# Average pooling over 512 MB: each 64 KB-per-partition load issued as two DMAs of half its columns

## The chip, the cores and the metric

The kernel runs on one core of one Trainium2 chip. The metric is the device time of one execution in microseconds (us). Three executions of the kernel before took 1558.53, 1558.62 and 1558.92 us, so its time is the median, 1558.62 us.

## The reference

The input x is a float32 array of 64 x 256 x 8192 elements (536.87 MB). Each output element is the mean of four neighbouring elements of the last axis, and the windows do not overlap:

```
kernel_size = stride = 4
out_len = (length - kernel_size) // stride + 1          # 2048
for i in range(out_len):
    start = i * stride
    output[:, :, i] = np.mean(x[:, :, start : start + kernel_size], axis=2)
```

The output is 64 x 256 x 2048 float32 (134.22 MB). Since 8192 is a multiple of 4, no window crosses a row, and the whole input may be treated as one flat run of numbers, of which every four make one output.

## The kernel before, in words

The flat input is cut into 32 groups. In a group, each of the 128 partitions owns one unbroken run of 32768 input elements (128 KB) and the 8192 outputs (32 KB) that come from it. A group is worked in two steps, so there are 64 steps, counted here from load 0 to load 63.

One step loads half of every partition's run: 16384 columns, 64 KB per partition, 8.39 MB in all, into a tile `xt` (line 70). The tiles `xt` come from a pool with two buffers, so load n+2 goes to the buffer of load n and cannot be issued before VectorE (DVE) has read that buffer for the last time. All DMAs, loads and stores alike, are issued by SyncE (SP) on one queue, in program order: an issue that waits holds up every issue behind it. Each DMA is carried out by 16 DMA engines side by side, each of which moves 8 of the 128 partition rows, one packet per row.

The work on a tile is the helper `pool`. DVE adds neighbouring pairs and writes the sums into the front half of the same tile (line 51), then adds neighbouring sums into the output tile `ot` (line 56). ScalarE (ACT) multiplies that part of `ot` by a quarter in place (line 57). The output tiles have two buffers of their own. One store of 4.19 MB, 32 KB per partition, writes a whole group (line 74). It is issued one group late: SP issues the store of group g-1 right behind the second load of group g. So from the second group on the queue holds, again and again: load, load, store.

The last step differs. Its load is issued as two DMAs of 11264 and 5120 columns (`LAST`), DVE and ACT work on the two pieces separately, and the outputs of the last group leave in three stores (lines 76 and 81). These two loads are called the tail pieces below.

The program that is built counts the completion of DMAs on eight semaphores in turn. The issue of a DMA therefore also waits until the DMA eight places before it has completed.

Of the kernel before, what the change touches and what calls it, by code (L numbers as in the profile page):

```python
# [1 line left out]

# [4 lines left out]

ADD = mybir.AluOpType.add

LOAD = 16384  # L10
PER_STORE = 2
LAST = (11264, 5120)


@with_exitstack
def kernel(
    ctx: ExitStack,
    tc: tile.TileContext,
    x: bass.AP,
    kernel_size: bass.AP,  # L20
    stride: bass.AP,
    out: bass.AP,
):

    nc = tc.nc
    K = int(kernel_size)
    assert K == 4 and int(stride) == 4 and x.shape[-1] % 4 == 0
    P = nc.NUM_PARTITIONS  # L30
    dt = x.dtype
    inv_k = 1.0 / K

    run = LOAD * PER_STORE
    total = x.shape[0] * x.shape[1] * x.shape[2]
    groups = total // (P * run)
    assert groups * P * run == total and groups >= 2
    xg = x.flatten_outer_dims().rearrange("r l -> (r l)").rearrange("(g p w) -> g p w", p=P, w=run)
    og = out.flatten_outer_dims().rearrange("r l -> (r l)").rearrange(
        "(g p w) -> g p w", p=P, w=run // K  # L40
    )

    pin = ctx.enter_context(tc.tile_pool(name="xin", bufs=2))
    pout = ctx.enter_context(tc.tile_pool(name="res", bufs=2))

    def pool(xt, at, width, ot, to):


        half = width // 2
        four = xt[:, at : at + width].rearrange("p (m k) -> p m k", k=2)  # L50
        nc.vector.tensor_tensor(  # L51
            out=xt[:, at : at + half], in0=four[:, :, 0], in1=four[:, :, 1], op=ADD
        )
        two = xt[:, at : at + half].rearrange("p (m k) -> p m k", k=2)
        o = ot[:, to : to + width // K]
        nc.vector.tensor_tensor(out=o, in0=two[:, :, 0], in1=two[:, :, 1], op=ADD)  # L56
        nc.scalar.mul(o, o, inv_k)  # L57

    tiles = {}
    for n in range(groups * PER_STORE):  # L60
        g, j = divmod(n, PER_STORE)
        last = n == groups * PER_STORE - 1
        if j == 0:
            tiles[g] = pout.tile([P, run // K], dt, name="ot")
        ot = tiles[g]
        xt = pin.tile([P, LOAD], dt)
        spans, at = [], 0
        for w in LAST if last else (LOAD,):
            lo = j * LOAD + at
            nc.sync.dma_start(out=xt[:, at : at + w], in_=xg[g][:, lo : lo + w])  # L70
            spans.append((at, w))
            at += w
        if j == PER_STORE - 1 and g > 0:
            nc.sync.dma_start(out=og[g - 1], in_=tiles.pop(g - 1)[:, :])
        if last:
            nc.sync.dma_start(out=og[g][:, : j * LOAD // K], in_=ot[:, : j * LOAD // K])
        for at, w in spans:
            to = (j * LOAD + at) // K
            pool(xt, at, w, ot, to)
            if last:  # L80
                nc.sync.dma_start(out=og[g][:, to : to + w // K], in_=ot[:, to : to + w // K])


# [1 line left out]
_INS = ['x', 'kernel_size', 'stride']  # L85
_OUTS = [((64, 256, 2048), 'float32')]

_NUMBERS = {'kernel_size': 4, 'stride': 4}


# [26 lines left out]
```

## Time and profile before

| What | Value |
|---|---|
| median of three executions | 1558.62 us |
| the profiled execution: its own time | 1558.32 us |
| the profiled execution: span from first to last instruction | 1556.5 us |
| moved by DMA | 671.12 MB, mean 431 GB/s |
| DVE busy | 839.8 us (54% of the span) |
| ACT busy | 232.9 us (15%) |

The profiled execution spends 1.82 us outside its span. Busy shares are averages over the whole span. Besides the views of the page, the trace keeps one record for each packet that a DMA engine handled: when it started, how long it took, and its size. A packet of a load here is one partition's 64 KB; a packet of a store is one partition's 32 KB; and each DMA ends on each of the 16 engines with one packet of 4 bytes that counts up its semaphore.

### The profile page before, as it was taken

To read this page: it belongs to the slowest core of one execution; us is meant where nothing else is said; L and a number is where in the kernel's file an instruction comes from. 1 tells how busy PE (TensorE), PEld (TensorE's weight loads), DVE (VectorE), ACT (ScalarE), POOL (GpSimd) and SP (SyncE) were. 2 spreads that over 40 slices of the span, in tenths; PEclk is the share of its full clock that TensorE was granted. 3 is DMA by queue.
4 is the path that set the end of the run, shared out by engine and by line. 5 is a ranking of instruction groups with operands and counts; after the bars stand their busy time and mean duration, and the time that the engine had idled before them with its cause. 6 is when DMAs were issued, how large, how long until landed. Compare 5 with 4: busy or idle time off the path is not lost.

```text
span 1556.5 us, 463 instructions
## 1 busy us (share of the span) xinstructions
DVE 839.8 (54%) x130; ACT 232.9 (15%) x66; POOL 0.2 (0%) x4
## 2 busy tenths in 40 slices
DVE  3645645456454564545645556545465454654546
ACT  1101111111111111111111111010110101101011
POOL 0000000000000000000000000000000000000000
DMA  9999999999999999999999999999999999999999
GB/s 416 445 406 431 431 435 440 431 429 433 423 441 433 431 431 425 440 431 431 435 436 435 437 435 435 428 432 435 431 433 440 428 441 436 433 431 425 440 429 389
DMA packets 14259, 671.12 MB, mean 431 GB/s; under 512 B 1584, under 2 KB 1584, under 8 KB 1712
## 3 DMA queue, kind: packets, MB, share of 16 engines
q1 hardware_dynamic: 14256, 671.09, 99.9%
q14 instruction: 3, 0.02, 0.0%
HBM read 536.87 MB, written 134.22 MB: 431 GB/s over the span
## 4 chain that ended last, share of the span: by engine, by line
DMA 72%; DVE 27%; issue 0%; ACT 0%; SPq 0%
DMA xt<-in_x_dram 72%; DVE xt L51 18%; DVE ot L56 9%; ACT ot L57 0%; SPq L70 0%
## 5 line engine op out<-in xcount | busy, mean ns | idle before, releaser
L51 DVE TENSOR_TENSOR xt<-xt 128x8192 f32<-128x8192 f32 (+1 forms) x65 | 556.5, 8561 | 699.9 <-DMA xt<-in_x_dram 699.8
L57 ACT ACTIVATE ot<-ot 128x4096 f32<-128x4096 f32 (+1 forms) x65 | 231.6, 3564 | 1311.2 <-DVE ot L56 1311.2
L56 DVE TENSOR_TENSOR ot<-xt 128x4096 f32<-128x4096 f32 (+1 forms) x65 | 283.4, 4360 | 3.9
L57 ACT ACT_TABLE_LOAD x1 | 1.3, 1283 | 0.7 <-PEq L98 0.7
L98 POOL MEMSET const-bfloat16-1.0<- 128x1 bf16 x1 | 0.1, 101 | 0.0
L98 POOL MEMSET const-uint8-127<- 128x1 uint8 x1 | 0.1, 101 | 0.0
L98 POOL MEMSET const-float32-0.0<- 128x1 f32 x1 | 0.1, 98 | 0.2 <-issue 0.2
L98 POOL MEMSET const-float32-1.0<- 128x1 f32 x1 | 0.1, 98 | 0.0
## 6 DMA issues: line engine op xcount, KB each, us to landing
out_dram<-ot SPq DMA_DIRECT2D x31, 4096.0 KB, 41.2
xt<-in_x_dram SPq DMA_DIRECT2D x1, 5632.0 KB, 29.1
xt<-in_x_dram SPq DMA_DIRECT2D x1, 2560.0 KB, 34.8
out_dram<-ot SPq DMA_DIRECT2D x1, 2048.0 KB, 17.1
out_dram<-ot SPq DMA_DIRECT2D x1, 1408.0 KB, 12.2
xt<-in_x_dram SPq DMA_DIRECT2D x63, 35.2
out_dram<-ot SPq DMA_DIRECT2D x1, 640.0 KB, 10.7
```

What stands on the lines that cost most here:

```text
L51: nc.vector.tensor_tensor(out=xt[:, at : at + half], in0=four[:, :, 0], in1=four[:, :, 1], op=ADD)
L56: nc.vector.tensor_tensor(out=o, in0=two[:, :, 0], in1=two[:, :, 1], op=ADD)
L57: nc.scalar.mul(o, o, inv_k)
L98: nc = _bacc.Bacc("TRN2", target_bir_lowering=False, num_devices=1)
```

## The change

Every load but the last one, which already consists of two DMAs, is issued as two DMAs, of columns 0 to 8191 and of columns 8192 to 16383 of the tile. The tile, its buffers, the sums, the multiplication and the stores stay as they were. DVE's first addition on a tile still covers all its 16384 columns, so it waits for both DMAs.

```diff
 LOAD = 16384
 PER_STORE = 2
+HALVES = (8192, 8192)
 LAST = (11264, 5120)
...
         xt = pin.tile([P, LOAD], dt)
-        spans, at = [], 0
-        for w in LAST if last else (LOAD,):
+        at = 0
+        for w in LAST if last else HALVES:
             lo = j * LOAD + at
             nc.sync.dma_start(out=xt[:, at : at + w], in_=xg[g][:, lo : lo + w])
-            spans.append((at, w))
             at += w
         if j == PER_STORE - 1 and g > 0:
             nc.sync.dma_start(out=og[g - 1], in_=tiles.pop(g - 1)[:, :])
         if last:
             nc.sync.dma_start(out=og[g][:, : j * LOAD // K], in_=ot[:, : j * LOAD // K])
-        for at, w in spans:
+        at = 0
+        for w in LAST if last else (LOAD,):
             to = (j * LOAD + at) // K
             pool(xt, at, w, ot, to)
             if last:
                 nc.sync.dma_start(out=og[g][:, to : to + w // K], in_=ot[:, to : to + w // K])
+            at += w
```

## The prediction

> **What bounds the kernel now.** I read the page's head first, for who is busy all the time.
>
> ```profile
> span 1556.5 us, 463 instructions
> DVE 839.8 (54%) x130; ACT 232.9 (15%) x66; POOL 0.2 (0%) x4
> DMA packets 14259, 671.12 MB, mean 431 GB/s; under 512 B 1584, under 2 KB 1584, under 8 KB 1712
> q1 hardware_dynamic: 14256, 671.09, 99.9%
> ```
>
> No compute engine is near full, but the packets of the one queue fill 99.9% of the time of 16 DMA engines. The kernel is bound by the time of its packets: 12672 of data and 1584 of 4 bytes (99 DMAs times 16).
>
> The chain of waits seems to tell another story, so I read it second:
>
> ```profile
> 1391.12 8.70 DVE xt L51
> ...
> 1399.84 4.43 DVE ot L56
> ...
> 1404.29 35.15 DMA xt<-in_x_dram
> ...
> 1439.47 8.70 DVE xt L51
> ```
>
> Here DVE is on the path for 13.15 us of each 48.35. But that is only the path of one buffer. A load takes 35.15 us from issue to landing because it stands in the queue behind the rest of the other load and, in half of the cases, a store. The question is how much work is queued when a load is issued, and the order of time answers it:
>
> ```profile
> 1439.47 8.69 DVE L51 TENSOR_TENSOR xt<-xt 128x8192 f32<-128x8192 f32 x1 [6.14 <-DMA xt<-in_x_dram]
> 1448.19 4.42 DVE L56 TENSOR_TENSOR ot<-xt 128x4096 f32<-128x4096 f32 x1
> 1452.65 0.33 SPq L70 DMA_DIRECT2D xt<-in_x_dram  x1
> 1452.65 3.62 ACT L57 ACTIVATE ot<-ot 128x4096 f32<-128x4096 f32 x1 [15.68 <-DVE ot L56]
> 1456.30 0.34 SPq L74 DMA_DIRECT2D out_dram<-ot  x1
> 1468.47 8.69 DVE L51 TENSOR_TENSOR xt<-xt 128x8192 f32<-128x8192 f32 x1 [15.85 <-DMA xt<-in_x_dram]
> ```
>
> The load issued at 1452.65 finds another load that lands only at 1468.47, so 15.8 us of work is still ahead of it. The tightest places are the starts, before there are stores: the load issued at 55.1 us finds 6.2 us of work (DVE sits idle 6.19 us, until 61.30). So the queue never runs dry, and a DMA's latency costs nothing; what a change does to the sum of packet times comes out one to one.
>
> Third, the rate by stage, with the boundaries laid on landings (81.72, 617.41 and 1487.82 are starts of L51 in the chain, each behind the second load of a group):
>
> ```profile
> 81.72:617.41 535.69, 288.60 (x44) 79.55 (x22) 0.00 (x0) 1.00 1.00 432
> 617.41:1487.82 870.41, 472.22 (x73) 130.18 (x36) 0.00 (x0) 1.00 1.00 434
> ```
>
> In the second stage 18 rounds of load, load, store take 870.41 us, 48.356 each. In the first stage 11 rounds take 535.69 us, 3.77 more than 11 x 48.356, though the DMA share is 1.00 in both. By the packet records the 3.77 us sit in single slow packets, mostly the last load packet ahead of a store, which take 2.5 to 3.6 us instead of 2.418 on most engines about once per round, and nearly cease after some 740 us.
>
> **What a packet costs.** The packet records of the same execution give durations by size. Load packets of 64 KB: 2418 ns at the least and in most cases. Store packets of 32 KB: 1213. The tail pieces' load packets: 45056 bytes 1665 at the least, 1668.7 on average; 20480 bytes 761 and 764.3. The semaphore packets: 9. A data packet starts 4 ns before the one ahead of it on its engine has ended (3 ns beside a semaphore packet), so from start to start these are 2414, 1209 and 6 ns. Two packets of 32 KB thus take 2 x 1209 - 2414 = 4 ns more than one of 64 KB: a packet has a small fixed cost.
>
> The records also time whole DMAs, as the mean over the engines from one DMA's semaphore packet to the next one's. After 620 us, a load behind a store takes 19.320 us, a load behind a load 19.346, mean 19.333; a store takes 9.684. Check: 19.320 + 19.346 + 9.684 = 48.350, against the 48.356 above. The tail pieces take 13.328 and 6.093.
>
> **The change part by part.**
>
> *Packets and semaphores, on the bounding path.* 63 loads become 126 DMAs. That adds 63 x 16 = 1008 semaphore packets and 63 x 128 = 8064 data packets; on each engine, 9 packets per load. No row shows a 32 KB load, so I bound it per split load. From below by the store, which has the size but the other direction: 2 x 9.684 - 19.333 = +35 ns. From above by the tail pieces, which have the direction and are one load in two DMAs: 13.328 + 6.093 - 19.333 = +88 ns. Times 63: +2.2 to +5.5 us. Within this I build from the floor and the excess over it. The floor for half a load is 8 x 1209 + 6 = 9678 ns. The excess per packet of the tail pieces is 3.3 ns (20480 bytes) and 4.2 (45056) while DVE works, which it does nearly all through these two loads, and 1.3 while it does not. In the rounds DVE works during 3.5 us of the first and 13.15 of the second load, 43% of 38.7. So 0.43 x 3.7 + 0.57 x 1.3 = 2.3 ns, half a load takes 9678 + 8 x 2.3 = 9696 ns, and a split load 19.393 us, +60 ns. Times 63 this is **+3.8 us**. I take it because it goes by load packets, at the rounds' own mix.
>
> *The slow packets of the first stage* come at the turn from loads to stores, and the turns remain. I leave their 3.77 us as they are; bounds are that they vanish (-3.8) or double (+3.8), as the records do not say what makes or ends them.
>
> *SP's issues.* 63 more at 0.33 us each, 20.7 us of SP, which waits far longer:
>
> ```profile
> SPq L70 <- DVE ot L56: 817.2, 62, 13.2
> SPq L70 <- DMA xt<-in_x_dram: 549.3, 62, 21.0
> SPq L74 <- ACT ot L57: 101.9, 31, 3.3
> ```
>
> The second half is issued 0.33 us behind the first, whose 9.7 us of packets cover it. A store behind it waits for ACT's 3.62 us in any case (3.3 us in the third row) and loses nothing to 0.33. On the path of the end: 0.
>
> *The eight semaphores.* Five instead of three DMAs per round use them up faster. I went through the new order: what stands eight places ahead of an issue is always a DMA queued ahead of load n when load n+2 is issued, or load n itself or older (the first half of load 7, for example, waits for store 0, queued ahead of load 4). The issue waits for DVE's work on load n anyway, so the new waits are over by then: 0. If one were not, it would first eat the 6.2 or 15.8 us of queued work.
>
> *DVE's wait* for two DMAs instead of one: the second half lands last, where the whole load landed before. SP's extra wait instructions on line 70 are 17 ns each; one such on DVE per tile is covered by the 6.14 to 15.9 us that it sits idle: 0. ACT, the stores and the tail are untouched.
>
> **Sum.** 1558.32 + 3.8 = 1562.1 us for an execution like the profiled one. The median of the runs shown stands 0.30 above the profiled one, so I predict 1562.4 us, 0.24% slower.
>
> **A rule against the rows.** The Trainium skill, "DMA: Bandwidth & Descriptors", section "Anatomy of one DMA", gives a DMA a fixed cost of about 2.0 us beside its bytes and puts most of it down to the confirmation of the last write; the page measured it on GpSimd's path. Paid for each of the 63 added DMAs it would be an estimated +126 us, 1684 us in all. The row that bears on it is the spacing of queued DMAs here: between a load's last data packet and the next DMA's first on an engine lie a few ns, so such a cost is overlapped as long as the queue holds work. [...] The halves step by 128 KB from row to row, as the loads do already, and the tail's 20 KB pieces at that pitch ran at 20480 B / 764.3 ns = 26.8 GB/s per engine against 27.1 for whole loads.
>
> **The rivals.**
> 1. *The slow packets go away* (not slower). Half-size packets shift the engines against each other, and the first stage runs like the second. For it: the stage did end by itself, and the spread of one DMA's semaphore packets over the engines grew from 0.5 us to 3 in that time. Against: nothing ties the ending to packet size. It gives 3.8 - 3.8 = 0, 1558.6 us; from 0.7 us saved the outcome is within 0.2%.
> 2. *They grow or last.* Doubled they give 1566.2 us; going on through the 20 later rounds at 3.77 / 11 = 0.34 us each they add 6.9 us: 1569.3 us. For it: 16 engines that stay in step. Against: 18 rounds without.
> 3. *The queue runs dry at the half's boundary.* The first load landed 21.9 us after issue where queued ones take 19.33, so an exposed start costs some 2.6 us; 63 of them make 1726 us. Against: the cover above.
> 4. *The change does not do what it says.* If engines cut 64 KB up already, nothing moves but 63 x 6 ns = 0.4 us: 1559.0. Against: the records show single packets of 65536 bytes.
>
> **How the numbers follow.** 0.2% of 1558.6 us is 3.1 us, about what a measurement here can tell from no change; the forecast's +3.8 stands close above it. Forecast with its bounds (+2.2 to +5.5, 1560.8 to 1564.1): 0.68, of which I put 0.57 above 3.1 and 0.11 below. Rival 1: 0.16, same. Rival 2: 0.09, slower. Rivals 3 and 4: 0.01 each. Left for a gain that I can't name: 0.05 (rival 1 with the lowest packet cost gives 2.2 - 3.8 = -1.6 us, still within 0.2%). Together: slower 0.67, same 0.28, faster 0.05. The range leaves out the lower half of rival 1 and the gains below, and the upper half of rival 2 above: 1558.2 to 1567.0.
>
> **What would show it.** Right: the queue's packets rise from 14256 to 14256 + 8064 + 1008 = 23328 at 99.9%; rounds after 620 us of 48.36 + 0.12 = 48.48 us; load packets at 1213 to 1217 ns; DVE's busy time unchanged; its waits for loads 3 to 6 us longer in total. Wrong: a DMA share under 99%, a late round far from 48.48, or a first stage whose excess over its late rounds is not near 3.8 us.

## The result and the profile after

The changed kernel takes 1562.41 us (median of 10 executions, 1561.64 to 1562.74), the kernel before 1558.46 us on the same chip (median of 10, 1557.76 to 1558.95). The ratio is 1.0025 with a 95% interval of 1.0017 to 1.0034: slower by a quarter of a percent. The profiled execution after has a span of 1560.3 us and took 1562.08; before it was 1556.5 and 1558.32.

The head of the page after, with the DMA lines:

```profile
span 1560.3 us, 591 instructions
DVE 839.8 (54%) x130; ACT 233.0 (15%) x66; POOL 0.2 (0%) x4
DMA packets 23333, 671.14 MB, mean 430 GB/s; under 512 B 2592, under 2 KB 2592, under 8 KB 2720
q1 hardware_dynamic: 23328, 671.10, 100.0%
```

The compute engines did the same work, the queue's packets rose from 14256 to 23328, and their time still fills the span. The bound did not move. DVE's idle time in front of its loads grew by 3.9 us in total (columns: us in total, times, longest us; before, then after):

```profile
DVE xt L51 <- DMA xt<-in_x_dram: 699.8, 63, 22.6
DVE xt L52 <- DMA xt<-in_x_dram: 703.7, 63, 22.6
```

The order of time for one round shows that the queue did not run dry either:

```profile
1112.24 4.43 DVE L57 TENSOR_TENSOR ot<-xt 128x4096 f32<-128x4096 f32 x1
1116.70 0.80 SPq L71 DMA_DIRECT2D xt<-in_x_dram  x2
1116.70 3.62 ACT L58 ACTIVATE ot<-ot 128x4096 f32<-128x4096 f32 x1 [15.66 <-DVE ot L57]
1120.35 0.34 SPq L74 DMA_DIRECT2D out_dram<-ot  x1
1132.69 8.69 DVE L52 TENSOR_TENSOR xt<-xt 128x8192 f32<-128x8192 f32 x1 [16.02 <-DMA xt<-in_x_dram]
```

The two issues take 0.80 us together, end before ACT has finished, and the store is issued right after ACT, as before. The other load lands only at 1132.69, so 16 us of work lay ahead of the halves when they were issued.

The stages, with the boundaries on landings as in the prediction:

```profile
81.94:616.94 535.00, 288.60 (x45) 79.58 (x22) 0.00 (x0) 1.00 1.00 432
616.94:1491.56 874.62, 472.23 (x72) 130.22 (x36) 0.00 (x0) 1.00 1.00 432
```

The first 11 rounds of load, load, store take 535.00 us, 0.69 less than before. The next 18 take 874.62, 4.21 more. The start (up to the landing of load 3) and the end add 0.22 and 0.06. These four make the 3.8 us between the spans. So the kernel lost more in its regular rounds than the total shows, and gained a part of it back where the slow packets had been.

The packet records, averaged over the 16 DMA engines, separate this better, because a landing follows the slowest engine alone:

| Mean over the engines | before | after |
|---|---|---|
| late round (median of the last 14 of 28) | 48.350 us | 48.504 us |
| what the 28 rounds take above 28 late ones | 2.50 us | 1.39 us |
| end of the last packet on the slowest engine, behind the mean engine | 1.75 us | 1.95 us |

### The profile page after: what moved, and what is told of

The parts are those of the page before. It is cut to its first block, busy times and chain, and to the rows that moved or that the text cites. A ratio compares the mean times of both kernels' runs of the same rounds, so it can differ in the third digit from the quotient of the medians.

```text
span 1560.3 us, 591 instructions
## 1 busy us (share of the span) xinstructions
DVE 839.8 (54%) x130; ACT 233.0 (15%) x66; POOL 0.2 (0%) x4
## 3 DMA queue, kind: packets, MB, share of 16 engines
q1 hardware_dynamic: 23328, 671.10, 100.0%
## 4 chain that ended last, share of the span: by engine, by line
DMA 71%; DVE 27%; SPq 1%; issue 0%; ACT 0%; DVEq 0%
DMA xt<-in_x_dram 71%; DVE xt L52 18%; DVE ot L57 9%; SPq L71 1%; ACT ot L58 0%; DVEq L52 0%
```

## The experiments

The experiments ran on three chips on which the kernel before takes 1557.36, 1557.47 and 1557.46 us. Each run is compared with the kernel before on its own chip, not with 1558.46.

**Packets or DMAs?** The change doubles both. Theory P: what is paid for is the packet. Theory D: much of it is the DMA, by its semaphore packet and by something that happens where one load DMA follows another. Two kernels have the small packets without the added DMAs, in all loads but those of the last group (62 of 64). In each, step j takes every second piece of a partition's run, so that one DMA has rows that are broken up in DRAM; the results go to the matching parts of `ot`. With `SEGS = 2`:

```diff
+        segs = g < groups - 1
+        if segs:
+            nc.sync.dma_start(
+                out=xt[:, :].rearrange("p (a w) -> p a w", a=SEGS),
+                in_=xg[g].rearrange("p (a j w) -> p a j w", a=SEGS, j=PER_STORE)[:, :, j, :],
+            )
...
+        two = xt[:, :half].rearrange("p (a m k) -> p a m k", a=SEGS, k=2)
+        o = ot[:, :].rearrange("p (a j m) -> p a j m", a=SEGS, j=PER_STORE)[:, :, j, :]
```

> One DMA per load again, but its packets are of 32 KB: in groups 0 to 30, step j takes the two 8192-column pieces j and j+2 of each partition's run, so a row is two separate pieces in DRAM; the sums go to the matching quarters of the output tile. 62 loads. Theory P (the cost belongs to packets: 4 ns for each added one, and some 4 ns more for each load packet beyond the first sixteen behind a store): 32 + 34 = 66 ns per load, 4.1 us, less about 0.9 that the changed kernel gains in the first stage: near 1561.7 us, late rounds of 48.49 us. Theory D (beyond 4 ns per packet the cost belongs to the DMA: a semaphore packet and a slowdown that starts where one load DMA follows another): 32 ns per load, 2.0 us, less 0.9: 1559.5 to 1560.5 us, late rounds of 48.42 us.

Measured: 1561.48 us against 1557.36, ratio 1.0026 (1.0016 to 1.0035). That is 4.1 us more, where theory P gave 3.2 and theory D 1.0 to 2.0. The page has the packets of the changed kernel but the semaphores of the one before:

```profile
DMA packets 22195, 671.12 MB, mean 430 GB/s; under 512 B 1584, under 2 KB 1584, under 8 KB 1712
q1 hardware_dynamic: 22192, 671.09, 99.9%
```

Late rounds take 48.501 us, in the changed kernel 48.504. Theory P's 48.49 holds, theory D's 48.42 does not: with the DMAs undone and the packets kept, the whole cost stays. The rounds decide here, as the totals also hold the start, the slow packets and the end.

With `SEGS = 4`:

> As the run with one DMA and 32 KB packets, with four pieces of 4096 columns per load: 16 KB packets. Theory P: 32 packets of 607 ns from start to start per engine give 112 ns per load, and the slowdown per packet some 100 more: 212 x 62 = 13.2 us, near 1571 us, late rounds of 48.78 us. Theory D: 112 x 62 = 6.9 us, near 1565 us, late rounds of 48.58 us.

Measured: 1569.15 us, ratio 1.0076 (1.0064 to 1.0089), late rounds of 48.802 us. Again theory P's 48.78 and not theory D's 48.58. The total alone would not have told: it lies between theory P's 1571 and theory D's 1565, because the slow packets, treated below, cost less here. The next kernel makes the same 16 KB packets with four DMAs per load:

```diff
-HALVES = (8192, 8192)
+HALVES = (4096, 4096, 4096, 4096)
```

> The changed kernel with four DMAs of 4096 columns for each load but the last: the same 16 KB packets as the run with one DMA and 16 KB packets, and three more DMAs per load. Theory P: three semaphore packets of 6 ns more per load than that run, 63 x 18 ns = 1.1 us above it, near 1572.5 us. Theory D: three boundaries of about 40 ns more per load, 7.6 us above it. Both give some 14 us above the kernel before.

Measured: 1570.34 us, ratio 1.0083 (1.0069 to 1.0097), 1.2 us above the run with one DMA. Both pages count their packets:

```profile
DMA packets 38067, 671.12 MB, mean 428 GB/s; under 512 B 1584, under 2 KB 1584, under 8 KB 1712
q1 hardware_dynamic: 38064, 671.09, 100.2%
```

```profile
DMA packets 41478, 671.16 MB, mean 428 GB/s; under 512 B 4608, under 2 KB 4608, under 8 KB 4736
q1 hardware_dynamic: 41472, 671.11, 100.2%
```

The first fence is the page of the run with one DMA per load, the second that of the run with four. The 1.2 us are about what theory P gave (1.1), but not for its reason. The late rounds are the same, 48.802 and 48.797 us, though there are six more DMAs in each. In the profiled executions the mean engine ends at 1564.75 and 1564.79 us; what differs is the slowest engine, 1.07 us behind the mean in the one and 2.37 in the other. In the rounds an added DMA costs nothing that can be seen.

The three sizes make a line. Per round and engine there are 24, 40 and 72 data packets of loads and store, and a round takes 48.350, 48.50 and 48.80 us. That is 9.5 ns per added packet between the first two and 9.3 between the last two.

**What the 9.5 ns are.** Between two sizes, 4 ns are the fixed cost of a packet: 2 x 1209 - 2414 from start to start. The rest is in the excess of load packets over their least duration. I put the late load packets in order of their place behind the last store (ns above 2418 and above 1213, means over engines and rounds):

```
64 KB packets (before):  first load   0.0 0.0 0.0 0.0 0.0 0.1 0.4 1.0
                         second load  1.0 1.0 2.4 3.0 3.5 3.7 3.8 4.9
32 KB packets (after):   load, 1st half 0.0 0.0 0.1 0.6 0.1 0.3 0.5 0.7
                         load, 2nd half 0.7 1.0 2.6 3.0 4.0 4.7 4.2 3.9
                         next, 1st half 3.3 2.2 2.7 3.8 4.4 4.5 4.2 4.1
                         next, 2nd half 3.5 2.0 2.6 3.9 4.4 4.3 7.1 6.4
```

The first eight load packets behind a store have next to no excess, and the next eight climb to about 4 ns. From there on it stays near 4 ns, but falls back to about 2 on the second packet of each further DMA (places 18 and 26 in the changed kernel, place 18 alone in the run with one DMA and 32 KB). In these rounds the climb goes by the number of packets, not by time or bytes: it begins at the same places with 64 KB and with 32 KB, though that is 19 us behind the store in the one and 10 in the other. In the run with one DMA and 32 KB packets it begins at the same place too, so it does not need a DMA's boundary. The falls explain why added semaphore packets don't show: a late round's excess sums to 96 ns in the changed kernel and 113 with one DMA of the same packets, to 201 with four DMAs of 16 KB and 229 with one. These 17 and 28 ns less stand against two and six semaphore packets more of 6 ns each.

The place is not the whole of it. In the kernel before, the packets at places 11 to 16 average only 0.0 to 0.6 ns in the rounds that end between 230 and 760 us (slow packets left out), and near 3.5 only after some 900 us; in the changed kernel the packets from place 13 on have 1.2 to 3.9 ns in the earlier stretch as well. What decides that is not known. Nor does the excess follow DVE: the load packets of the changed kernel that ran wholly beside DVE averaged 2.6 ns of excess, those that ran wholly without DVE 2.8.

Runs that leave out the stores of the first 31 groups, and so most of the output, test whether the store is what resets it, and at the same time whether the slow packets of the first stage belong to stores:

```diff
-            nc.sync.dma_start(out=og[g - 1], in_=tiles.pop(g - 1)[:, :])
+            tiles.pop(g - 1)
```

> The kernel before without the stores of groups 0 to 30, so most of the output is left out. Question 1, the slow packets of the first stage. Theory T (they belong to the turn from loads to stores): none behind the first packets, two loads take the same time from the start. Theory S (they belong to the first 700 us of an execution, whatever runs): load packets of 2.5 us and more keep coming until some 700 us. Question 2, the few ns that load packets take above their floor: if a store resets them and they rise with the packets since, each packet is 4 to 5 ns above the floor of 2418 throughout, and two loads take 2 x (8 x 2418.3 + 6) = 38.70 us. Whole run near 1254 us.

> The changed kernel without the stores of groups 0 to 30. Two loads take 2 x (16 x 1213.2 + 12) = 38.85 us if all packets stand 4.2 ns above their floor, 0.15 us more than in the loads-only run with 64 KB packets, as in the kernels with stores (48.50 against 48.35). If the semaphores of the extra DMAs are free, as one and four DMAs at 16 KB suggested, 38.84. Whole run near 1259 us.

Measured: 1257.68 us with 64 KB and 1262.97 with 32 KB. Both are some 4 us above the expected totals; the spacing of the loads is what the question rests on. Two lines of the chain of waits of each, 64 KB first; the columns are start, duration and what:

```profile
907.63 25.50 DMA xt<-in_x_dram
...
946.33 25.50 DMA xt<-in_x_dram
```

```profile
911.19 25.20 DMA xt<-in_x_dram
...
950.03 25.22 DMA xt<-in_x_dram
```

Two loads take 946.33 - 907.63 = 38.70 us and 950.03 - 911.19 = 38.84 us, the expected numbers. The path runs through every second load, so from one line to the other two loads pass. After the first 300 us, load packets stand 3.8 ns (64 KB) and 4.2 ns (32 KB) above their least duration on average: without stores, the excess is there all the time. Why load packets behave so remains open.

**The slow packets.** In the loads-only run with 64 KB, 62 load packets were more than 2% above 2418 ns, 40 of them in the first 100 us, of which 16 are the first packet of each engine; three came after 300 us. In the kernel before there were 176, and more than 20 in every 100 us up to 600. Theory T holds for the most part: they belong to the turn from a load to a store, but for some at the very start. The next run asks whether they need engines that are in step, by putting some engines behind with four small loads ahead of the first:

```diff
+        if n == 0:
+            p0 = 0
+            for rows in (8, 4, 2, 1):
+                nc.sync.dma_start(out=ot[p0 : p0 + rows, :4096], in_=xg[0][p0 : p0 + rows, :4096])
+                p0 += rows
```

> The kernel before with four small loads of 8, 4, 2 and 1 rows of 16 KB ahead of the first load, into an output tile that is overwritten later: they put engine 0 about 2.4 us behind engines 8 to 15, engine 1 1.8, engines 2 and 3 1.2, engines 4 to 7 0.6. Theory K (the slow packets of the first stage need engines that are in step): the first twelve rounds lose their 2.4 us over 48.35 each; 0.6 us for the small loads and about 1 us for an engine that ends later come on top: 0.5 to 1.5 us below the kernel before. Rival (the slow packets have another cause and go on as they did): 1 to 2 us above it.

Measured: 1559.91 us, ratio 1.0017 (1.0008 to 1.0026). That is 2.4 us above the kernel before; the rival had 1 to 2 above, theory K 0.5 to 1.5 below. But the rounds speak for theory K: the first twelve together take 0.35 us more than 12 x 48.35, where the kernel before takes 2.40 more. The slow packets did mostly go. What ate the gain was the start and the end. The first load lands, on the mean engine, at 25.25 us against 21.99, where I expected 0.6 us; and the slowest engine ends 3.35 us behind the mean, 1.60 more than before. DVE's first addition, in the kernel before and here, shows the start on the slowest engine:

```profile
22.63 8.69 DVE L51 TENSOR_TENSOR xt<-xt 128x8192 f32<-128x8192 f32 x1 [22.63 <-DMA xt<-in_x_dram]
28.39 8.69 DVE L51 TENSOR_TENSOR xt<-xt 128x8192 f32<-128x8192 f32 x1 [28.39 <-DMA xt<-in_x_dram]
```

The second try puts the small loads behind load 1 (`if n == 2`, ahead of load 2's tile):

> The four small loads of the skewed kernel, but issued behind load 1, where the queue holds work, so that the first load is not late by 3.3 us as there. Theory K (the slow packets need engines that are in step): the first twelve rounds lose some 2.0 of their 2.4 us; 0.56 us for the small loads and about 1.4 us for a slowest engine that ends further behind the mean (2.8 us in the skewed run against 1.4 before) come on top: within 0.5 us of the kernel before. If the 3.3 us of the start did not account for the skewed run's loss, 2 us above it again.

Measured: 1560.06 us against 1557.46, ratio 1.0016 (1.0007 to 1.0025): 2.6 us above and not within 0.5. The first twelve rounds lose even more of their excess (0.18 us is left), but the small loads delay load 2 by 3.5 us on the mean engine here too. By the records their 16 KB packets take 0.7 to 1.7 us instead of the 0.611 of a 16 KB store packet, and while they run, most first packets of load 2 take 4 to 5.2 us instead of 2.418. The small loads all go to partitions 0 to 14; whether that is the reason wasn't tried.

**The cover taken away.** The prediction costs the added DMAs' latency at nothing because work is always queued. With one input buffer, no load is queued while DVE works:

```diff
-    pin = ctx.enter_context(tc.tile_pool(name="xin", bufs=2))
+    pin = ctx.enter_context(tc.tile_pool(name="xin", bufs=1))
```

> The changed kernel with one input buffer instead of two, so that the queue holds no load while DVE works: the cover is taken away. A load then costs 19.39 us of packets, 13.15 us of DVE and the latency of a DMA that nothing covers. With 2.6 us, from the first load's landing of the kernel before: 35.1 us per load, near 2260 us in all. The second half's DMA follows the first in the queue, so against the run with one buffer and 64 KB it costs only its packets, 0.06 us per load, 4 us. If each DMA had an own latency there, 2 us and more per load, 130 us.

> The kernel before with one input buffer, to set beside the changed kernel with one buffer (2283.67 us, 23.2 and 21.8 us of DVE's idle time per load). If the second half's DMA costs only its packets even where nothing covers a DMA's latency: 63 x 0.06 = 4 us below that, near 2280 us. If each DMA had a latency of its own of 2 us and more: some 130 us below, near 2150 us. Every turn from a load to a store should show slow last load packets here too, since the engines set out together at each load.

Measured: 2283.67 us with halves and 2282.88 with whole loads, one run of each. The lines of the order of time are, first with halves and then with whole loads, DVE's last work on a tile and its first on the next:

```profile
1029.27 4.43 DVE L57 TENSOR_TENSOR ot<-xt 128x4096 f32<-128x4096 f32 x1
...
1055.45 8.69 DVE L52 TENSOR_TENSOR xt<-xt 128x8192 f32<-128x8192 f32 x1 [21.76 <-DMA xt<-in_x_dram]
```

```profile
1029.89 4.43 DVE L56 TENSOR_TENSOR ot<-xt 128x4096 f32<-128x4096 f32 x1
...
1056.21 8.69 DVE L51 TENSOR_TENSOR xt<-xt 128x8192 f32<-128x8192 f32 x1 [21.89 <-DMA xt<-in_x_dram]
```

With halves DVE sits idle 21.76 us, and the packets of a load are 19.4 of them: 2.4 us per load, SP's issue among them, are latency that now shows. That is close to the 2.0 us of the Trainium skill ("DMA: Bandwidth & Descriptors", section "Anatomy of one DMA"), which the page measured on another path. Of the 2.4 us about 1.1 pass before the first packets start, and these first packets take some 1.8 us each where 1.213 is the rule. With whole loads DVE's idle time is 21.89 us. So the latency is paid per exposed wait and not per DMA: the 63 added DMAs cost 0.8 us in all, where a latency for each would have cost some 130 and their packets alone 4. Why it is less than 4 was not followed up. Here the engines set out together at each load, their semaphore packets lie 0.3 to 1.0 us apart, and in the rounds that I followed, some 1000 us in, the last two 32 KB packets of the load ahead of a store took 1.3 to 2.3 us on most engines where 1.213 is the rule. The slow packets do not cease here, as expected for engines that are kept in step: up to 2200 us every load ahead of a store ends with about 31 of them with halves, two per engine, and with 16 or 17 with whole loads, one per engine, while the other loads have hardly any behind their first packets. DVE's idle time is 23.2 us on every second load with halves, 1.4 more than on the others. These are the loads with a store queued behind them. The expectation, near 2260 us, had left them out, and the time lies 24 us above it.

## Why the prediction was right

The number was right (1562.4 forecast, 1562.41 measured). The way to it was right in its bound and wrong in two sizes that offset each other, so that it agrees so closely is luck.

- *The bound.* Packet time goes into the end one to one, and all that was costed at nothing (SP's issues, the eight semaphores, DVE's wait, the latency) stayed hidden. DVE's waits for loads grew by 3.9 us in total, within the 3 to 6 forecast. Shown by the 100.0%, by the order of time above, and for the latency by the pair with one buffer.
- *Packets and semaphores: +3.8 us, measured about +4.9.* A late round grew by 0.154 us where the step said 0.12; a split load costs 77 ns, not 60, within the bounds of 35 and 88. The term that was mis-sized is the excess per packet. The prediction weighed it by DVE's share of the time; in the late rounds it goes by the place behind the last store instead, and the added packets mostly fall where it is full. The upper bound, from the tail pieces, was nearer: they too come far behind a store. The 6 ns for an added semaphore packet are offset by the lower excess behind each further DMA's start.
- *The slow packets: left at 3.77 us, measured 1.1 us less on the mean engine.* This step failed, and by a sign that the prediction itself had named: the first stage takes 535.00 us, 1.5 and not 3.8 above 11 late rounds of 48.504. Their size, too, was read from landings, which follow the slowest engine; on the mean engine it was 2.50 us, and 1.39 after. Smaller packets shrink it further: 0.69 and 0.44 us in the runs with one DMA and 32 or 16 KB packets. So rival 1 came true in part, but not for its reason. That slow packets cease once engines are out of step has support from the two skewed runs and the two with one buffer. Smaller packets, however, did not put the engines out of step sooner: near 500 us one DMA's semaphore packets lie 2.6 us apart in the kernel before, 1.4 in the changed one and 0.9 with one DMA and 16 KB packets. Load packets more than 48 ns above their least duration are as many as before in the changed kernel (181 against 176) and come until some 900 us, but they are shorter: 3.0 us per engine in sum against 4.2. With 16 KB packets they are 43, with 0.9 us in sum. Why a smaller packet loses less is open.
- *Start and end.* Not in the sum. On the mean engine load 3 lands 0.24 us later, but its four split loads are in the 4.9 already with 0.31; the slowest engine ends 0.20 us further behind the mean. So 4.9 - 1.1 - 0.1 + 0.2 make 3.9, against the 3.8 between the spans.
- *The rule of 2 us per DMA* did not add to the time, for the reason given: a queued DMA's latency is covered.
- *Rivals 2, 3 and 4* are out: the slow packets came for some 200 us longer but cost less in all, the queue did not run dry, and the packets were split.

## What to carry to other kernels

Where one queue's packets fill the DMA engines for the whole span, cost a change by packets and not by DMAs: here each added load packet per engine cost about 9.5 ns, which is 0.3% of a round for the step from 64 to 32 KB and 0.6% more for the step to 16 KB, and added DMAs cost next to nothing while the queue held work. First find how much queued work lies ahead of an issue; here it was 6 us and more, and latency and issue time cost nothing. And when a total agrees, still compare it stage by stage, since two misjudged terms may hide each other.

## What the runs showed of the hardware that was not expected

- The excess of load packets in late rounds (next to none in the first eight behind a store, about 4 ns by the sixteenth), at the same places for packets of 64 and 32 KB, and its absence in the kernel before from 230 to 760 us.
- The turn from loads to stores: the last load packets take up to 1.2 us longer (with one input buffer up to 1.6) when the 16 engines are in step, and hardly any longer once they are some 3 us apart. With 16 KB packets in one DMA they are few though the engines never get further than 1.8 us apart.
- The end is set by the slowest DMA engine, 1.1 to 3.3 us behind the mean one in the runs with stores and two input buffers. Skewing the engines cured 2.1 to 2.2 us of slow packets and lost 1.2 to 1.6 us of that at the end, apart from what the small loads cost. No version faster than both kernels came out of it; the rounds of the kernel before take 2.5 us, or 0.16% of the time, above late ones in all, and that is what there is to gain.
